# Three of seven quarter products with the operand's high and low parts side by side: one 512-column matmul for both, VectorE adds the halves

## The chip, the cores and the metric

The kernel runs on one core of one Trainium2 chip. The metric is the device time of one launch in microseconds (us). The engines have short names here: PE is TensorE (PEld its loading of weights), DVE is VectorE, ACT is ScalarE, POOL is GpSimd, SP is SyncE, which starts most transfers. PE works in 128 x 128 weights against a moving operand of up to 512 columns, and writes into eight PSUM banks of 512 fp32 columns each.

## The reference

Two decoder layers on a sequence of 512 tokens of width 1024. Each layer is a SwiGLU feed-forward block at half weight, a mixer (a convolution, a sliding-window attention and an attention to 256 memory tokens), a second feed-forward block at half weight, and a norm:

```python
def swiglu(x, w1, w3, w2):
    return (jax.nn.silu(x @ w1) * (x @ w3)) @ w2

for l in range(DEPTH):
    h = x + 0.5 * swiglu(rms_norm(x, ffn1_norm[l]), ffn1_w1[l], ffn1_w3[l], ffn1_w2[l])
    ...
    h = h + 0.5 * swiglu(rms_norm(h, ffn2_norm[l]), ffn2_w1[l], ffn2_w3[l], ffn2_w2[l])
    x = rms_norm(h, final_norm[l])
```

DEPTH is 2, D_MODEL 1024, D_FF 2816; all in fp32. The mixer, which adds to h between the two blocks, is left out here. The change lies in `x @ w1` and `x @ w3` of the four feed-forward blocks.

## The kernel before

**Numbers in two parts.** Each fp32 operand is split into a high part (a ScalarE copy into the fp32r type, L146) and a low part (VectorE subtracts the high part from the number, L147). `mm3` (L178 to L180) makes a product of two such operands by three matmuls into the same PSUM tile: high weight with high operand, high weight with low operand, low weight with high operand. Weights come as `raw` tiles by DMA from SP's queue; `pair()` gives the tiles `whi` and `wlo`, of which there are four of each.

**A feed-forward block.** The 2816 columns are 22 blocks of 128. The first four blocks are formed directly (matmuls of 512 columns into mm banks), the other 18 as nine pairs of blocks by `up_pair` (L358 to L420), a scheme of seven products of quarters in the place of eight: the contraction of 1024 is halved (two halves of four steps of 128) and the tokens are halved (QT = 256 columns). `Seven` (L295 to L343) prepares the token side once for a block: products 1, 2 and 6 take their operands from `mh` and `ml`, made by `first()`, products 3, 5, 7 and 4 from `xhi` and `xlo`, made by `rest()`; the sums of quarters are made at L321 (tile `msum`), then split: `plain` splits a quarter, `cut` a sum. Over the weight side `up_pair` loops: for both matrices (w1 and w3, index i) it splits a unit of weights, and runs two products on it, in the groups 1 and 2, 6 and 3, 5 and 7, and last product 4 for both. A product is four steps of `mm3` with 256 columns, twelve matmuls.

**Where products lie.** There are three mm banks, one cf bank, two po banks and two pt banks. In `up_pair` the list `xy` has two po banks, one for each matrix: product 1 in the left half of xy[i], product 2 in the right half; one ScalarE copy of 512 columns (L392) brings both into the SBUF tile `part[i]`, and VectorE adds them into `u` or `g` (L386, in the function `add`). Products 6 and 5 are later accumulated onto the left half of xy[i] (they start without `start`), each copied into `part[i]` by ScalarE (L400, L405). The list `zv` has two pt banks: product 3 in the left half of zv[i], products 7 and then 4 in the right. After 7, one VectorE add of 512 columns (L407 calls `add`) brings both halves into u or g with product 5's copy; after 4 one of 256. SiLU (L414), product (L415) and the split of the result (L418, L419) follow. Since `add` records its operation at one line, all of these adds, and the two that form sums of weights in `raw`, carry L386.

**Order.** `ffn` runs through QUARTERS, (0,6), (6,6), (12,6), (18,4): the stages q0 to q3 hold two, three, three and one pairs (q0 also has the four direct blocks, made ahead), each followed by a down projection of those columns, which adds into h at L506. There are four blocks, so 36 pairs. The order of the instructions on each engine isn't written by hand: a scheduler decides it from the dependencies of the program and a few `issue_after` hints, and each engine then runs its list in order, with semaphore waits. A tile or bank that is written again waits for its last readers; the program tracks a PSUM bank as one thing, so a write to its one half waits for a reader of the other.

Of the kernel before, what the change touches and what calls it, by code (L numbers as in the profile page):

```python
# [11 lines left out]
F32R = mybir.dt.float32r  # L12
I32 = mybir.dt.int32
AF = mybir.ActivationFunctionType
ALU = mybir.AluOpType
AX = mybir.AxisListType
ALL = slice(None)

P = 128
D = 1024  # L20
S = 512
# [44 lines left out]
def trunk(ctx: ExitStack, tc: tile.TileContext, xT, memT, pos, w1a, w3a, w2a, w1b, w3b, w2b,  # L66
          wconv, wqk, wvm, wmem, wout, gains, small, rows, consts, out):
    nc = tc.nc
    V, G, A, T = nc.vector, nc.gpsimd, nc.scalar, nc.tensor

    const = ctx.enter_context(tc.tile_pool(name="const", bufs=1))
    res = ctx.enter_context(tc.tile_pool(name="res", bufs=1))
# [7 lines left out]
    turn, tail, hold = [0], [None], {}  # L80
# [10 lines left out]
    def bank(shape, tag):  # L91

        if tag == "mm":
            return ps_mm.tile(shape, F32, tag=tag, name=tag)
        return ps_ax.tile(shape, F32, tag=tag, name=tag, bufs=1 if tag == "cf" else 2)

    def tm(name, tag="t", bufs=None):
        return tmp.tile([P, S], F32, tag=tag, name=name, **({"bufs": bufs} if bufs else {}))
# [4 lines left out]
    def raw_tile(src, cols):  # L103
        raw = wst.tile([P, UNIT], F32, tag="raw", name="raw", bufs=3)
        nc.sync.dma_start(raw[:, 0:cols], src)
        return raw
# [5 lines left out]
    first = []  # L112
# [32 lines left out]
    def split(hi, lo, x, on):  # L145
        a = A.activation(hi, x, AF.Copy)  # L146
        return a, on.tensor_tensor(out=lo, in0=x, in1=hi.bitcast(F32), op=ALU.subtract)  # L147
# [29 lines left out]
    def mm3(ps, a, b, first, last, **more):  # L177
        T.matmul(ps, a[0], b[0], start=first, stop=False, **more)  # L178
        T.matmul(ps, a[0], b[1], start=False, stop=False, **more)  # L179
        tail[0] = T.matmul(ps, a[1], b[0], start=False, stop=last, **more)  # L180

    def at(p, *idx):
        return tuple(x[idx] for x in p)

    def blk(k, n=P):
        return slice(k * n, (k + 1) * n)
# [57 lines left out]
    class Stat:  # L244


        def __init__(self, tag, n=S, on=None):
            self.sums, self.tag, self.n, self.on = [], tag, n, on
# [18 lines left out]
    def operand():  # L267
        return (res.tile([P, KD, S], F32R, tag="xhi", name="xhi"), res.tile([P, KD, S], F32R, tag="xlo", name="xlo"))
# [16 lines left out]
    QT = 256  # L285
# [9 lines left out]
    class Seven:  # L295


        def __init__(self, n):
            self.n = n
            self.m = {}  # L300

        def quarter(self, half, i, t):

            return self.n[2 * half + i][:, :, blk(t, QT)]

        def first(self):
            near = (res.tile([P, 3, 4, QT], F32R, tag="nsh", name="mh"), res.tile([P, 3, 4, QT], F32R, tag="nsl", name="ml"))
            for i, j in enumerate((1, 2, 6)):
                self.m[j] = at(near, ALL, i)
            self.plain(1, 0, 0)  # L310
            self.plain(2, 1, 0)
            f = self.sum((0, 1), (1, 1), ALU.subtract)
            self.sum(f, (0, 0), ALU.subtract, f)
            self.cut(6, f)
# [7 lines left out]
            return out  # L322

        def plain(self, j, half, t):
            for i in range(2):
                hi, lo = at(self.m[j], ALL, blk(i, 2))
                split(hi, lo, self.quarter(half, i, t), V)

        def cut(self, j, f):
            hi, lo = (x.rearrange("p k t -> p (k t)") for x in self.m[j])  # L330
            split(hi, lo, f, V)

        def rest(self):
            far = tuple(x.rearrange("p k (u t) -> p (k u) t", t=QT) for x in operand())
            for i, j in enumerate((3, 5, 7, 4)):
                self.m[j] = at(far, ALL, blk(i, 4))
            self.plain(3, 1, 1)
            self.cut(5, self.sum((0, 0), (0, 1), ALU.subtract))
            f = self.sum((1, 1), (0, 1), ALU.subtract)
            self.cut(7, f)  # L340
            self.sum(f, (0, 0), ALU.add, f)
            self.sum(f, (1, 0), ALU.subtract, f)
            self.cut(4, f)  # L343
# [5 lines left out]
    def gated():  # L349
        p = gated_pair()  # L350
        return [at(p, ALL, i, ALL) for i in range(2)]

    def unit(x):
        p = pair()
        split(p[0], p[1], x, V)
        return p

    def up_pair(l, w13, f, M):  # L358

        raw = [raw_tile(w13[i][l, f], D) for i in range(2)]  # L360
        X = []
        for i in range(2):

            x = wst.tile([P, UNIT], F32, tag="aux", name="wsum", bufs=3)
            nc.sync.dma_start(x.rearrange("p (f c) -> p f c", f=2), w13[i][l, f : f + 2, :, 0:QW].rearrange("f p c -> p f c"))
            G.dma_start(x, w13[i][l, f + 1], accum_op=ALU.add)
            X.append(x)
        z = wst.tile([P, UNIT], F32, tag="raw", name="raw", bufs=3)
        for i in range(2):
            nc.sync.dma_start(z[:, blk(i, QW)], w13[i][l, f + 1, :, QW:])  # L370
        xy = [bank([P, S], "po") for _ in range(2)]
        zv = [bank([P, S], "pt") for _ in range(2)]
        x0, x1 = blk(0, QT), blk(1, QT)

        def product(ps, w, half, j, first=False):


            for k in range(4):
                mm3(ps, at(w, ALL, blk(4 * half + k)), at(M.m[j], ALL, k), first and k == 0, k == 3, skip_group_check=True)

        u, g = (tmp.tile([P, 2, S], F32, tag=t, name=t, bufs=n) for t, n in (("u", 1), ("g", 2)))
        part = [tm("part", "sq", 2) for _ in range(2)]
        to = (u, g)

        def add(out, a, b):
            V.tensor_tensor(out=out, in0=a, in1=b, op=ALU.add)  # L386

        for i in range(2):
            w = unit(raw[i])
            product(xy[i][:, x0], w, 0, 1, first=True)  # L390
            product(xy[i][:, x1], w, 1, 2)
            A.activation(part[i], xy[i], AF.Copy)  # L392
            add(to[i][:, 0, x0], part[i][:, x0], part[i][:, x1])

            add(raw[i][:, 0:QW], raw[i][:, 0:QW], X[i][:, QW:])
            add(raw[i][:, QW:], raw[i][:, QW:], raw[i][:, 0:QW])
        for i in range(2):
            w = unit(raw[i])
            product(xy[i][:, x0], w, 0, 6)
            A.activation(part[i][:, x1], xy[i][:, x0], AF.Copy)  # L400
            product(zv[i][:, x0], w, 1, 3, first=True)
        for i in range(2):
            w = unit(X[i])
            product(xy[i][:, x0], w, 1, 5)
            A.activation(part[i][:, x0], xy[i][:, x0], AF.Copy)  # L405
            product(zv[i][:, x1], w, 0, 7)
            add(to[i][:, :, x1], zv[i].rearrange("p (n t) -> p n t", n=2), part[i][:, x0].unsqueeze(1).to_broadcast([P, 2, QT]))  # L407
        w = unit(z)
        for i in range(2):
            product(zv[i][:, x1], w, i, 4)  # L410
            add(to[i][:, 1, x0], zv[i][:, x1], part[i][:, x1])
        out = gated()
        for n, sign in enumerate((1.0, -1.0)):
            A.activation(u[:, n], u[:, n], AF.Silu, scale=sign)  # L414
        M.gated = V.tensor_tensor(out=g, in0=g, in1=u, op=ALU.mult)  # L415
        for n, sign in enumerate((1.0, -1.0)):
            hi, lo = out[n]
            A.activation(hi, g[:, n], AF.Copy, scale=sign)  # L418
            V.scalar_tensor_tensor(out=lo, in0=g[:, n], scalar=sign, in1=hi.bitcast(F32), op0=ALU.mult, op1=ALU.subtract)  # L419
        return out  # L420

    def ffn(l, w13, w2, x, sums, factors, last, at_product, aside=None, closing=None):
# [55 lines left out]
        for q, (f0, nf) in enumerate(QUARTERS):  # L478
            ahead = 2 if q + 1 < len(QUARTERS) else 0
            for f in range(f0, f0 + nf + ahead, 2):  # L480
                if f not in g:
                    g[f], g[f + 1] = up_pair(l, w13, f, M)
                    if f == PLAIN:
                        with tc.issue_after(M.gated.ins):
                            rescale = after()
# [615 lines left out]
    for l in range(L):  # L1101
        x, new = nxt.x, Stat("st")
# [163 lines left out]
```

## Time and profile before

| what | value |
|---|---|
| median of 3 runs | 1763.83 us (1762.75 to 1764.15) |
| the profiled execution | 1764.53 us |
| its span, first to last instruction | 1762.8 us |
| granted clock of TensorE | 0.998 |
| matmuls of 256 columns by the pt lines (L178 to L180) | 864 of each line |
| hardware DMA queue | 190.45 MB, 35.4% of 16 engines |
| software DMA queue | 61.35 MB, 19.4% of 16 engines |

All times of instructions are from the one profiled execution. A row of the timeline has the start, the duration, the engine, the line, the operation, and what goes out and in, and in square brackets the idle time of the engine before it with what ended it. A row of a group has the count, the busy time in total, the mean in ns of one, and the idle time before the group with its releasers. A row of the waits of PE has the total, how often, and the longest. Matmuls overlap in the pipeline, so that one row's duration is longer than the distance to the next.

### The profile page before, as it was taken

How to read it: one execution, taken by the hardware profiler on the slowest of the kernel's cores; microseconds unless marked ns; L12 is line 12 of the kernel's file. 1: busy time of each engine (PE TensorE's matmuls, PEld its weight loads, DVE VectorE, ACT ScalarE, POOL GpSimd, SP SyncE). 2: the span in 40 equal slices, each digit the busy share in tenths (PEclk: the TensorE clock that was granted, in tenths of full speed). 3: DMA queues.
4: the chain of work that ended last, by engine and by line, in shares of the span. 5: the costliest groups of instructions: out<-in, count | busy, mean ns of one | idle time of the engine just before them, and what ended most of it. 6: DMA issues, size and time to landing. Idle time of an engine off the chain costs nothing.

```text
span 1762.8 us, 28084 instructions
## 1 busy us (share of the span) xinstructions
PE 1746.5 (99%) x11004; PEld 1576.7 (89%) x11004; DVE 1281.3 (73%) x1898; ACT 900.7 (51%) x1373; POOL 195.6 (11%) x220
## 2 busy tenths in 40 slices
PE   8999999999999999999999999999999999999998
PEld 7989999988888989898889898989888889998987
DVE  7968666589877757575677786666898677665756
ACT  6646444355765535353655463444467654353533
POOL 1001000006121000000010010000251310000000
PEclk9999999999999999999999999999999999999999
DMA  9456645257257546465567465642671766474622
GB/s 285 120 162 171 181 133 149 65 159 177 72 105 170 146 140 170 131 166 140 155 139 183 129 181 142 168 132 79 164 172 36 155 144 166 134 185 116 169 81 84
DMA packets 97205, 253.60 MB, mean 144 GB/s; under 512 B 9904, under 2 KB 16304, under 8 KB 97072
## 3 DMA queue, kind: packets, MB, share of 16 engines
q1 hardware_dynamic: 78064, 190.45, 35.4%
q0 software_dynamic: 19008, 61.35, 19.4%
q8 instruction: 86, 1.41, 0.3%
q14 instruction: 47, 0.39, 0.1%
HBM read 249.67 MB, written 2.10 MB: 143 GB/s over the span
## 4 chain that ended last, share of the span: by engine, by line
PE 98%; DVE 1%; DMA 1%; ACT 0%; issue 0%; SPq 0%; DVEq 0%; ACTq 0%
PE mm L178 14%; PE mm L179 14%; PE mm L180 14%; PE po L178 9%; PE po L179 9%; PE po L180 9%; PE pt L178 6%; PE pt L179 6%; PE pt L180 6%; PE po L870 2%; PE mm L818 1%; PE cf L178 1%; PE cf L180 1%; PE cf L179 1%; PE pt L859 1%; DMA raw<-in_w2b 1%
## 5 line engine op out<-in xcount | busy, mean ns | idle before, releaser
L146 ACT ACTIVATE whi<-raw 128x1024 fp32r<-128x1024 f32 (+3 forms) x346 | 326.2, 946 | 440.9 <-PE mm L179 219.9
L147 DVE TENSOR_TENSOR wlo<-raw,whi 128x1024 fp32r<-128x1024 f32 (+3 forms) x346 | 376.0, 1088 | 118.9 <-ACT whi L146 118.0
L179 PE MATMUL mm<-glo,whi 128*128 128x512 f32 (+1 forms) x752 | 292.1, 388 | 0.0
L178 PE MATMUL mm<-ghi,whi 128*128 128x512 f32 (+1 forms) x752 | 291.8, 390 | 0.0
L180 PE MATMUL mm<-ghi,wlo 128*128 128x512 f32 (+1 forms) x734 | 284.9, 388 | 0.0
L178 PE MATMUL pt<-xhi,whi 128*128 128x256 f32 x864 | 243.3, 283 | 1.4 <-DVE g L386 1.4
L180 PE MATMUL po<-mh,wlo 128*128 128x256 f32 x864 | 244.5, 283 | 0.0
L179 PE MATMUL po<-ml,whi 128*128 128x256 f32 x864 | 244.5, 283 | 0.0
L178 PE MATMUL po<-mh,whi 128*128 128x256 f32 x864 | 244.4, 283 | 0.0
L180 PE MATMUL pt<-xhi,wlo 128*128 128x256 f32 x864 | 243.9, 283 | 0.0
L179 PE MATMUL pt<-xlo,whi 128*128 128x256 f32 x864 | 243.9, 283 | 0.0
L506 DVE SCALAR_TENSOR_TENSOR h<-mm,h 128x512 f32<-128x512 f32 x126 | 86.3, 688 | 132.0 <-PE mm L180 131.9
L178 PEld LDWEIGHTS pt<-xhi,whi 128*128 128x128 f32 x864 | 165.2, 192 | 2.4 <-DVE g L386 1.6
L178 PEld LDWEIGHTS mm<-ghi,whi 128*128 128x128 f32 x752 | 141.4, 188 | 28.8 <-DVE h L506 1.2
L179 PEld LDWEIGHTS pt<-xlo,whi 128*128 128x128 f32 x864 | 165.7, 192 | 0.8
L178 PEld LDWEIGHTS po<-mh,whi 128*128 128x128 f32 x864 | 165.8, 192 | 0.7
L179 PEld LDWEIGHTS po<-ml,whi 128*128 128x128 f32 x864 | 165.8, 192 | 0.6
L179 PEld LDWEIGHTS mm<-glo,whi 128*128 128x128 f32 x752 | 141.3, 188 | 27.5
L180 PEld LDWEIGHTS po<-mh,wlo 128*128 128x128 f32 x864 | 165.8, 192 | 0.0
L180 PEld LDWEIGHTS pt<-xhi,wlo 128*128 128x128 f32 x864 | 165.7, 192 | 0.0
L180 PEld LDWEIGHTS mm<-ghi,wlo 128*128 128x128 f32 x734 | 137.8, 188 | 28.5
L1000 DVE SCALAR_TENSOR_TENSOR there<-ypad,par,there 128x512 f32<-128x512 f32 x180 | 136.0, 779 | 1.3
(334 smaller groups left out, 3322.0 us busy)
## 6 DMA issues: line engine op xcount, KB each, us to landing
raw<-in_w2a SPq DMA_DIRECT2D x48, 384.0 KB, 3.5
raw<-in_w2b SPq DMA_DIRECT2D x48, 384.0 KB, 3.6
raw<-in_w1b SPq DMA_DIRECT2D x26, 512.0 KB, 3.6
raw<-in_w3b SPq DMA_DIRECT2D x26, 512.0 KB, 3.7
raw<-in_w1a SPq DMA_DIRECT2D x25, 512.0 KB, 3.6
raw<-in_w3a SPq DMA_DIRECT2D x25, 512.0 KB, 4.0
wsum<-in_w1a SPq DMA_DIRECT2D x18, 512.0 KB, 4.4
wsum<-in_w3a SPq DMA_DIRECT2D x18, 512.0 KB, 4.3
```

What stands on the lines that cost most here:

```text
L146: a = A.activation(hi, x, AF.Copy)
L147: return a, on.tensor_tensor(out=lo, in0=x, in1=hi.bitcast(F32), op=ALU.subtract)
L178: T.matmul(ps, a[0], b[0], start=first, stop=False, **more)
L179: T.matmul(ps, a[0], b[1], start=False, stop=False, **more)
L180: tail[0] = T.matmul(ps, a[1], b[0], start=False, stop=last, **more)
L506: added = V.scalar_tensor_tensor(out=h[:, d, :], in0=ps, scalar=0.5, in1=h[:, d, :], op0=ALU.mult, op1=ALU.add)
L818: tail[0] = T.matmul(pp[i][:, z, :], q, k, start=not masked, stop=True, skip_group_check=True)
L859: tail[0] = T.transpose(pt[:, i, j, :], pr[:, i, blk(j)], ident)
L870: tail[0] = T.matmul(po[:, 2 * c + i, :], ptb[:, i, j, :], v, start=(j == 0), stop=(j == nk - 1))
L1000: V.scalar_tensor_tensor(out=cv[:, c, :], in0=ypad[:, c, j : j + S], scalar=conv_w[:, c, j : j + 1], in1=cv[:, c, :], op0=ALU.mult, op1=AL ...
```

## The change

The token operands are laid out anew: for each step of 128 the high part and the low part of the 256 columns lie next to each other, in one tile. Products 2, 7 and 4 use a new function `beside`: for each step one matmul of 512 columns, high weight with high and low operand side by side (the line L392 of the changed kernel), and one of 256, low weight with high operand (L390), onto the left half. The result takes a whole bank, whose halves VectorE adds (`summed`, two adds; for product 7 a ScalarE copy and an add). Products 1, 6, 3 and 5 are made as before, by `mm3`. Product 7 now comes ahead of 5 in the program.

Since a wide product takes a whole bank, the banks are shared anew: one pt bank `x` holds products 1, 6 and 5 of both matrices, each matrix in one half; one pt bank `c` holds product 3 of both; the po banks are for product 2 and for 7 with 4. In the changed kernel the ScalarE copies are L408 (product 1), L419 (product 6), L428 (product 5) and L425 (product 7), and all adds are L399.

```diff
         def first(self):
-            near = (res.tile([P, 3, 4, QT], F32R, tag="nsh", name="mh"), res.tile([P, 3, 4, QT], F32R, tag="nsl", name="ml"))
+            near = [res.tile([P, 6, 2, QT], F32R, tag=t, name=n) for t, n in (("nsh", "mh"), ("nsl", "ml"))]
...
         def cut(self, j, f):
-            hi, lo = (x.rearrange("p k t -> p (k t)") for x in self.m[j])
-            split(hi, lo, f, V)
+            z = self.whole[j]
+            split(z[:, :, 0], z[:, :, 1], f.rearrange("p (k t) -> p k t", k=4), V)
...
-        xy = [bank([P, S], "po") for _ in range(2)]
-        zv = [bank([P, S], "pt") for _ in range(2)]
+        x = bank([P, 2, QT], "pt")
...
+        def beside(ps, w, half, j, first=False):
+            for k in range(4):
+                (hi, lo), m = at(w, ALL, blk(4 * half + k)), M.m[j][k]
+                for n in (1, 0) if k == 3 else (0, 1):
+                    if n:
+                        T.matmul(ps[:, 0], lo, m[:, 0], start=False, stop=False, skip_group_check=True)
+                    else:
+                        tail[0] = T.matmul(ps, hi, m, start=first and k == 0, stop=k == 3, skip_group_check=True)
...
+        def summed(out, ps, a):
+            add(out, ps[:, 0], a)
+            add(out, out, ps[:, 1])
+
         for i in range(2):
             w = unit(raw[i])
-            product(xy[i][:, x0], w, 0, 1, first=True)
-            product(xy[i][:, x1], w, 1, 2)
-            A.activation(part[i], xy[i], AF.Copy)
-            add(to[i][:, 0, x0], part[i][:, x0], part[i][:, x1])
+            product(x[:, i], w, 0, 1, first=not i)
+            A.activation(part[i][:, x0], x[:, i], AF.Copy)
+            y = bank([P, 2, QT], "po")
+            beside(y, w, 1, 2, first=True)
+            summed(to[i][:, 0, x0], y, part[i][:, x0])
...
+        c, v = bank([P, 2, QT], "pt"), []
         for i in range(2):
             w = unit(raw[i])
-            product(xy[i][:, x0], w, 0, 6)
-            A.activation(part[i][:, x1], xy[i][:, x0], AF.Copy)
-            product(zv[i][:, x0], w, 1, 3, first=True)
+            product(x[:, i], w, 0, 6)
+            A.activation(part[i][:, x1], x[:, i], AF.Copy)
+            product(c[:, i], w, 1, 3, first=not i)
         for i in range(2):
             w = unit(X[i])
-            product(xy[i][:, x0], w, 1, 5)
-            A.activation(part[i][:, x0], xy[i][:, x0], AF.Copy)
-            product(zv[i][:, x1], w, 0, 7)
-            add(to[i][:, :, x1], zv[i].rearrange("p (n t) -> p n t", n=2), part[i][:, x0].unsqueeze(1).to_broadcast([P, 2, QT]))
+            v.append(bank([P, 2, QT], "po"))
+            beside(v[i], w, 0, 7, first=True)
+            A.activation(to[i][:, 1, x1], v[i][:, 0], AF.Copy)
+            add(to[i][:, 1, x1], to[i][:, 1, x1], v[i][:, 1])
+            product(x[:, i], w, 1, 5)
+            A.activation(part[i][:, x0], x[:, i], AF.Copy)
+            add(to[i][:, 0, x1], c[:, i], part[i][:, x0])
+            add(to[i][:, 1, x1], to[i][:, 1, x1], part[i][:, x0])
         w = unit(z)
         for i in range(2):
-            product(zv[i][:, x1], w, i, 4)
-            add(to[i][:, 1, x0], zv[i][:, x1], part[i][:, x1])
+            beside(v[i], w, i, 4)
+            summed(to[i][:, 1, x0], v[i], part[i][:, x1])
```

How this moves the instructions shows at three places. The number behind a name tells one tile from the next of the same name; what stands in brackets is the engine whose semaphore the instruction waits for (Activation is ScalarE).

On PE, in the first stage q0, at the end of a pair's product 3 and the start of product 6 of the second matrix. Before (pt_532 is zv of the second matrix, po_530 its bank xy):

```order
L179 MATMUL pt_532<-xlo_495,whi_630 128x256
L180 MATMUL pt_532<-xhi_494,wlo_631 128x256
L178 MATMUL po_530<-mh_337,whi_630 128x256 [waits Activation_49]
L179 MATMUL po_530<-ml_338,whi_630 128x256
L180 MATMUL po_530<-mh_337,wlo_631 128x256
```

The same place in the changed kernel: the end of product 6 of the first matrix (weights whi_595) and all of product 6 of the second (whi_624), both in the bank x, pt_529, and then product 5 of the first (whi_653):

```order
L180 MATMUL pt_529<-ml_338,wlo_596 128x256
L178 MATMUL pt_529<-ml_338,whi_624 128x256 [waits Activation_49]
L179 MATMUL pt_529<-ml_338,whi_624 128x256
...
L179 MATMUL pt_529<-ml_338,whi_624 128x256
L180 MATMUL pt_529<-ml_338,wlo_625 128x256
L178 MATMUL pt_529<-xhi_494,whi_653 128x256 [waits Activation_49]
L179 MATMUL pt_529<-xhi_494,whi_653 128x256 [waits DVE_49]
```

Before, another bank's product lay between two products on one bank; now three products on x follow one another, and the second and the third wait for the ScalarE copy of the one just ahead.

On ScalarE at the same place, before (part_535 and part_536 are the tiles `part` of the two matrices):

```order
L392 ACTIVATE part_536<-po_530 128x512 [waits PE_49]
L400 ACTIVATE part_535<-po_529 128x256 [waits DVE_49,PE_49]
L146 ACTIVATE whi_719<-raw_526 128x1024 [waits DMAHW5_49,DMAHW4_49,PE_49]
L146 ACTIVATE xhi_494<-msum_505 128x1024 [waits DVE_49]
L146 ACTIVATE whi_779<-raw_758 128x1024 [waits DMAHW6_49,PE_49]
L400 ACTIVATE part_536<-po_530 128x256 [waits DVE_49,PE_49]
L405 ACTIVATE part_535<-po_529 128x256 [waits PE_49]
```

And in the changed kernel (part_532 and part_533 are the same two tiles):

```order
L408 ACTIVATE part_533<-pt_529 128x256 [waits PE_49]
L146 ACTIVATE whi_713<-raw_526 128x1024 [waits DMAHW4_49,DMAHW5_49,PE_49,Activation_49]
L419 ACTIVATE part_532<-pt_529 128x256 [waits PE_49]
L146 ACTIVATE xlo_495<-msum_505 128x4x256 [waits DVE_49]
L146 ACTIVATE whi_764<-raw_746 128x1024 [waits DMAHW6_49,PE_49,Activation_49]
L419 ACTIVATE part_533<-pt_529 128x256 [waits PE_49]
L428 ACTIVATE part_532<-pt_529 128x256 [waits PE_49,Activation_49]
```

A split of the next weights (1024 columns) stands now ahead of each of the two copies of product 6 (L419), and the split's own wait is for PE's last use of an older `whi` tile.

On PE again, in stage q2 of the first block, where one pair ends and the next begins. Before (po_2859 is xy of the next pair):

```order
L179 MATMUL pt_2620<-xlo_495,whi_2777 128x256
L180 MATMUL pt_2620<-xhi_494,wlo_2778 128x256
L178 MATMUL po_2859<-mh_337,whi_2867 128x256 [waits Activation_49]
L179 MATMUL po_2859<-ml_338,whi_2867 128x256
L180 MATMUL po_2859<-mh_337,wlo_2868 128x256 [waits DVE_49]
```

In the changed kernel (pt_2545 is the old pair's bank x, pt_2775 that of the next):

```order
L179 MATMUL pt_2545<-xhi_494,whi_2699 128x256
L180 MATMUL pt_2545<-xhi_494,wlo_2700 128x256
L178 MATMUL pt_2775<-mh_337,whi_2780 128x256 [waits Activation_49]
L179 MATMUL pt_2775<-mh_337,whi_2780 128x256
L180 MATMUL pt_2775<-mh_337,wlo_2781 128x256
```

The next pair's first product came after a product in another bank, and waited for weights; now it comes right behind product 5 of the old pair, in the same bank, and waits for the copy (L428) of that product.

More of the change, by code (lines that the diff above doesn't have):

```diff
@@ L299, in __init__ @@
             self.n = n
-            self.m = {}
+            self.m, self.ends, self.whole = {}, {}, {}
         def quarter(self, half, i, t):
@@ L306, in first @@
         def first(self):
-            near = (res.tile([P, 3, 4, QT], F32R, tag="nsh", name="mh"), res.tile([P, 3, 4, QT], F32R, tag="nsl", name="ml"))
+            near = [res.tile([P, 6, 2, QT], F32R, tag=t, name=n) for t, n in (("nsh", "mh"), ("nsl", "ml"))]
             for i, j in enumerate((1, 2, 6)):
-                self.m[j] = at(near, ALL, i)
+                self.m[j] = [near[b // 6][:, b % 6] for b in range(4 * i, 4 * i + 4)]
+                self.ends[j] = [near[b // 6][:, b % 6 : b % 6 + 2] for b in (4 * i, 4 * i + 2)]
+            self.whole[6] = near[1][:, 2:6]
             self.plain(1, 0, 0)
@@ L324, in plain @@
         def plain(self, j, half, t):
-            for i in range(2):
-                hi, lo = at(self.m[j], ALL, blk(i, 2))
-                split(hi, lo, self.quarter(half, i, t), V)
+            for i, z in enumerate(self.ends[j]):
+                split(z[:, :, 0], z[:, :, 1], self.quarter(half, i, t), V)
         def cut(self, j, f):
-            hi, lo = (x.rearrange("p k t -> p (k t)") for x in self.m[j])
-            split(hi, lo, f, V)
+            z = self.whole[j]
+            split(z[:, :, 0], z[:, :, 1], f.rearrange("p (k t) -> p k t", k=4), V)
         def rest(self):
-            far = tuple(x.rearrange("p k (u t) -> p (k u) t", t=QT) for x in operand())
+            far = [x.rearrange("p k (u t) -> p k u t", t=QT) for x in operand()]
             for i, j in enumerate((3, 5, 7, 4)):
-                self.m[j] = at(far, ALL, blk(i, 4))
+                z = self.whole[j] = far[i // 2][:, blk(i % 2, 4)]
+                self.m[j], self.ends[j] = [z[:, k] for k in range(4)], [z[:, 0:2], z[:, 2:4]]
             self.plain(3, 1, 1)
@@ L378, in product @@
             for k in range(4):
-                mm3(ps, at(w, ALL, blk(4 * half + k)), at(M.m[j], ALL, k), first and k == 0, k == 3, skip_group_check=True)
+                m = M.m[j][k]
+                mm3(ps, at(w, ALL, blk(4 * half + k)), (m[:, 0], m[:, 1]), first and k == 0, k == 3, skip_group_check=True)
+        def beside(ps, w, half, j, first=False):
[6 more added lines that the diff above has]
+                        tail[0] = T.matmul(ps, hi, m, start=first and k == 0, stop=k == 3, skip_group_check=True)
         u, g = (tmp.tile([P, 2, S], F32, tag=t, name=t, bufs=n) for t, n in (("u", 1), ("g", 2)))
```

## The prediction

> **What bounds the kernel now.** I read the page first, then the waits of PE, then busy time by stretch, and last the timeline.
>
> ```profile
> PE 1746.5 (99%) x11004; PEld 1576.7 (89%) x11004; DVE 1281.3 (73%) x1898; ACT 900.7 (51%) x1373; POOL 195.6 (11%) x220
> PE 98%; DVE 1%; DMA 1%; ACT 0%; issue 0%; SPq 0%; DVEq 0%; ACTq 0%
> PE mm L178 <- ACT xhi L156: 6.0, 1, 6.0
> PE pt L178 <- DVE g L386: 1.4, 1, 1.4
> ```
>
> The first two lines are from the page (busy time, and the chain of work that ended last); the other two are the two longest waits of PE. PE is busy for 1746.5 of 1762.8 us and the chain is 98% PE: the time is the sum of the matmuls, and every microsecond in which PE newly waits is added in full. Of the pairs' matmuls (tiles po and pt) one alone waited, for 1.4 us.
>
> Which engine comes next is a matter of the stage. The rows below give busy time in four stretches of pairs: stage q0 of the first FFN (two pairs), q1 of the same FFN (three), q2 (three, as ordinary stages look) and q0 of the second FFN.
>
> ```profile
> 54.70:92.50 37.80, 37.80 (x315) 37.68 (x314) 33.96 (x44) 24.00 (x34) 3.45 (x4) 1.00 0.59 160
> 139.40:202.40 63.00, 63.00 (x517) 62.52 (x516) 53.59 (x103) 37.25 (x59) 8.34 (x8) 1.00 0.69 175
> 232.70:295.80 63.10, 63.10 (x516) 62.56 (x516) 42.56 (x53) 33.62 (x49) 4.32 (x5) 1.00 0.67 170
> 577.20:614.90 37.70, 37.70 (x314) 37.61 (x313) 32.72 (x42) 23.53 (x34) 3.45 (x4) 1.00 0.58 143
> ```
>
> Behind the length of the stretch stand PE, the weight loads, VectorE, ScalarE and GpSimd, then the granted clock and the DMA share. VectorE has 34.0 of 37.8 us (90%) in q0 and 42.6 of 63.1 (67%) in q2; ScalarE has 24.0 and 33.6.
>
> **The matmuls that go.** PE's rows are pipelined, so the price of one is the distance between two starts.
>
> ```profile
> 66.00 0.28 PE L179 MATMUL po<-ml,whi 128*128 128x256 f32 x1
> 66.12 0.28 PE L180 MATMUL po<-mh,wlo 128*128 128x256 f32 x1
> 66.24 0.28 PE L178 MATMUL po<-xhi,whi 128*128 128x256 f32 x1
> ...
> 295.96 0.40 PE L178 MATMUL mm<-ghi,whi 128*128 128x512 f32 x1
> ...
> 297.35 0.39 PE L178 MATMUL mm<-ghi,whi 128*128 128x512 f32 x1
> ...
> 305.51 0.39 PE L178 MATMUL mm<-ghi,whi 128*128 128x512 f32 x1
> ```
>
> 256 columns take 0.120 us. The rows from 295.96 on are 512 columns wide, without a gap: 36 steps from 297.35 to 305.51, 0.227 us each, while the six right behind the change from narrow to wide (295.96 to 297.35) took 0.232. A step of a changed product was 3 x 0.120 = 0.360 us; wide and narrow in turn it is now 0.227 + 0.120 = 0.347 or 0.232 + 0.120 = 0.352, and saves 0.013 or 0.008. I take the middle, 0.010, since the trace has no such alternation. Products 2, 7 and 4, each for two matrices, with four steps: 24 steps in a pair, 864 in 36 pairs: **8.6 us** (6.9 to 11.2; 0 if the alternation costs more). Each step drops one instruction and no columns, 768 pass PE either way, and hence the gain is this small. The Trainium skill ("TensorE: Matmul & The Clock Gate", Back-to-back issue gap) gives for a single matmul at full clock N/2.4 + 2.5 ns, so 2.5 ns for the dropped instruction. By that, an estimate, the gain would be 864 x 2.5 ns = 2.2 us; the trace's 120 and 227 ns, at clock 1.00, speak for more: 3 x 120 - 227 - 120 = 13 ns.
>
> **The wait that is added.** Before, the products 1, 6 and 5 of matrix 1 and of matrix 3 lay in two po banks. Now both share one pt bank x, each in its half, and the program lets PE write the one half only when ScalarE has copied out the other. In the order, PE gets three products on x in a row in the first q0 (product 6, 6, 5), each with a wait for ScalarE. What stands behind such a wait on PE is everything: PE runs in order, so no matmul fills the gap.
>
> The price, by the shortest case, comes from four rows: from PE's last matmul to its reader, and from a reader's end to PE.
>
> ```profile
> 79.20 0.28 PE L180 MATMUL pt<-xhi,wlo 128*128 128x256 f32 x1
> 79.52 0.43 DVE L386 TENSOR_TENSOR u<-pt,part 128x256 f32<-128x256 f32 x1 [0.63 <-PE pt L180]
> ...
> 1492.96 0.68 DVE L386 TENSOR_TENSOR g<-pt,part 128x512 f32<-128x512 f32 x1
> 1493.69 0.39 PE L178 MATMUL pt<-xhi,whi 128*128 128x256 f32 x1 [1.38 <-DVE g L386]
> ...
> L400 ACT ACTIVATE part<-po 128x256 f32<-128x256 f32 x72 | 27.3, 381 | 69.2 <-PE po L180 68.1 <-DVE u L386 0.8 <-DVE g L386 0.3
> ```
>
> The reader starts 0.32 us after the last matmul's start; ScalarE's copy takes 0.38; PE starts 0.05 after its reader's end (1493.64). The next matmul would have started 0.12 after the last one, so the **short price** is 0.32 + 0.38 + 0.05 - 0.12 = 0.63 us. The trace shows the return path for VectorE alone; I take it for ScalarE too, with 0 and 0.3 as bounds, which moves 21 places by -1 and +5 us.
>
> Often ScalarE is not free. Its split of the next weights also waits for this product, but for the one before the last of its matmuls, so it gets in first. The trace of before has the very case:
>
> ```profile
> 66.32 1.06 ACT L146 ACTIVATE whi<-raw 128x1024 fp32r<-128x1024 f32 x1 [0.27 <-PE po L179]
> 67.28 0.37 ACT L400 ACTIVATE part<-po 128x256 f32<-128x256 f32 x1
> ```
>
> The product ended with the matmul of 66.12 above; its copy ended at 67.65. In before PE went on at 66.24 in another bank. Now it would go on at 67.65 + 0.05 = 67.70: the **long price** is 1.46 us.
>
> Places where a product on x follows directly the one whose copy it waits for: 21 in the order of the change, none before. Three stand in each of the four q0 stages, nine in the q1 and q2 stages, none in q3.
> - q0: in each stage two have the split of 1024 columns in front on ScalarE, one is bare: 4 x (2 x 1.46 + 0.63) = 14.2 us.
> - q1 and q2, eight stages: one direct place each, at the pair's end, bare (0.63); other products on x come four or eight steps behind their copy's product, where a split in front on ScalarE can cost from 0 to 0.83 (the long price less the short). I take 0.83 once in a stage, ScalarE being busy over half the time there: 8 x 1.46 = 11.7, and 0.6 for the ninth place: 12.3.
>
> The Trainium skill ("PSUM — Partial Sum Buffer", PSUM bank collisions raise a hardware error) says that two engines must never touch one bank's partitions at once, disjoint columns included, and that the wait is to be set by bank: by that rule the wait is no excess of the scheduler and speaks against this sharing; without it the sum would be the gain alone. No run here tests the collision.
>
> **What VectorE gets.** A pair had four adds of 256 columns and two of 512; now it has 14 of 256.
>
> ```profile
> 73.00 1.22 DVE L147 TENSOR_TENSOR wlo<-raw,whi 128x1024 fp32r<-128x1024 f32 x1
> 74.14 0.68 DVE L386 TENSOR_TENSOR g<-pt,part 128x512 f32<-128x512 f32 x1
> 74.74 0.68 DVE L386 TENSOR_TENSOR raw<-raw 128x512 f32<-128x512 f32 x1
> 75.33 1.22 DVE L147 TENSOR_TENSOR xlo<-msum,xhi 128x1024 fp32r<-128x1024 f32 x1
> ...
> L386 DVE TENSOR_TENSOR g<-part 128x256 f32<-128x256 f32 x36 | 15.0, 416 | 0.0
> ```
>
> A 512 add takes 0.60 of VectorE's time (74.14 to 74.74, 0.08 less than its row). The 256 add, 0.42, less the same 0.08, takes 0.34: 10 x 0.34 - 2 x 0.60 = 2.2 us more in a pair, 79 in all. In q2 that is 42.6 + 6.6 of 63: covered by PE. In q0 it is 34.0 + 4.4 = 38.4, against 37.8 - 0.6 + 3.6 = 40.8 with the new waits: VectorE just fits, but work before product 4's matmuls comes later. The low half of product 4's operand (75.33, ended 76.55) was needed by PE at 78.0, 1.45 us of room; four more adds stand ahead of it and PE is not later by more than two waits. I count 0.5 in each of two FFN1 q0 stages and 1.0 in q1 of the first FFN, where VectorE had 53.6 of 63.0 and gets 60.2: 2 us, bounds 0 and 12 (half of the adds of these eleven pairs, 11 x 1.1). Operands laid out hi beside lo are read and written in runs of 256; no row shows a difference, and none is counted (bounds +-0.1 us for each of 16 cuts, in VectorE's slack). ScalarE has four copies of 256 more and two of 512 less, 0.4 us in a pair, beside PE.
>
> **Sum.** 14.2 + 12.3 + 2.0 - 8.6 = +19.9 us on the profiled execution's 1764.5, which lies 0.7 above the runs' median of 1763.8: 1783.7, rounded down to 1783, since the 11.7 of q1 and q2 is an upper choice.
>
> **Rivals.** *All waits short.* ScalarE does the copies ahead of its splits, or the splits are held up by something else: 21 x 0.63 = 13.2 against 8.6, +4.6: 1768.4; with the gain at 11.2 it is +2.0 and 1765.8, no change that can be measured. For it: half the places are bare in the order. Against: the rows at 66.32 and 67.28.
> *The waits cost less than the matmuls save.* This is the case of faster: it decides at 8.6 / 21 = 0.41 us for a place (0.53 with the gain at 11.2). If the copies were out in time everywhere, 1763.8 - 8.6 = 1755.2, or 1752.6. For it: in before such copies never delayed PE, and the return path to PE is from a single row. Against: 0.38 of copy and 0.28 of the last matmul's own duration are in every place.
> *VectorE becomes the bound in q0 and in q1 of the first FFN.* If half of the 24 us of adds in these eleven pairs come uncovered, +12 less the 2 that are counted: 1783.7 + 10 = 1794. For it: 38.4 us of work in 40.8. Against: waits of PE and of VectorE overlap.
> *The wide matmul saves nothing* (a gain of 0): 1783.7 + 8.6 = 1792.
>
> **How the numbers follow.** Forecast, 1770 to 1791: 0.66. All waits short, 1763 to 1770: 0.12. Faster, 1750 to 1762: 0.12. VectorE or no gain, 1790 to 1803: 0.10. The time is that of the first: 1783. The range from 1764 to 1792 takes in the first, nearly all of the second and a little of the last, 0.80. A measurement of this kernel tells about 0.2% (3.5 us) from no change: faster 0.12, same 0.08, slower 0.80.
>
> **What would show it.** PE's waits after the change should name ScalarE's copies L408, L419 and L428 as releasers for pt, some 21 to 35 times, from 0.6 to 1.5 us, about 26 us in all; the wide-narrow step should repeat at 0.347 to 0.352; q0 stretches should grow to about 41 us and q3 stay. It is wrong if PE's idle time grows by under 9 us, if the waits name VectorE, or if the step is 0.360.

## The result and the profile after

| kernel | median, us | runs | ratio to before, 95% interval |
|---|---|---|---|
| before | 1763.42 (1762.75 to 1764.15) | 5 | |
| the change | 1812.62 (1810.34 to 1815.04) | 5 | 1.0278 [1.0263, 1.0293] |

The change is slower by 49 us. Its profiled execution took 1812.62 us, with a span of 1810.9. The page of the change, its busy time:

```profile
PE 1760.7 (97%) x10140; PEld 1536.0 (85%) x10140; DVE 1365.1 (75%) x2186; ACT 908.6 (50%) x1445; POOL 195.0 (11%) x220
```

PE has 864 matmuls fewer, as it should, VectorE 84 us more. PE stood idle for 1810.9 - 1760.7 = 50.2 us, where it was 16.3; the rest of the longer span counts as busy time, the slow matmuls of q3 that are shown below among it. The waits of PE in the change say for what it stood idle (total, times, longest):

```profile
PE mm L178 <- ACT ghi L441: 11.9, 4, 3.0
PE pt L178 <- ACT part L419: 8.4, 6, 1.6
PE pt L178 <- ACT part L428: 8.2, 13, 1.4
PE mm L178 <- ACT xhi L156: 6.3, 1, 6.3
PE pt L178 <- ACT part L408: 3.9, 9, 0.8
```

Lines 2, 3 and 5 are the waits on the shared bank x that were forecast: 28 times, 20.5 us. The first line was not: four waits of 3 us for `ghi`, the high part of a pair's result, and all four are in q3. The fourth line is the wait at the start, which was there before. Two more waits of 0.7 us each, in q0 of the third block, belong to the same kind: a small matmul of the norm takes its pt bank there between two products, and waits for product 5's copy (L428), and the next product waits for the copy of that matmul's result.

One look at two of the forecast places and at one in q3, from the timeline of PE in the change:

```profile
66.47 0.28 PE L180 MATMUL pt<-ml,wlo 128*128 128x256 f32 x1
68.10 0.39 PE L178 MATMUL pt<-ml,whi 128*128 128x256 f32 x1 [1.35 <-ACT part L419]
68.33 0.28 PE L179 MATMUL pt<-ml,whi 128*128 128x256 f32 x1
...
283.10 0.28 PE L180 MATMUL pt<-xhi,wlo 128*128 128x256 f32 x1
283.85 0.38 PE L178 MATMUL pt<-mh,whi 128*128 128x256 f32 x1 [0.47 <-ACT part L428]
...
359.29 0.40 PE L180 MATMUL mm<-ghi,wlo 128*128 128x512 f32 x1
362.67 1.23 PE L178 MATMUL mm<-ghi,whi 128*128 128x512 f32 x3 [2.99 <-ACT ghi L441]
363.70 0.63 PE L179 MATMUL mm<-glo,whi 128*128 128x512 f32 x1
364.13 0.63 PE L180 MATMUL mm<-ghi,wlo 128*128 128x512 f32 x1
...
366.26 0.55 PE L179 MATMUL mm<-glo,whi 128*128 128x512 f32 x1
366.65 0.39 PE L180 MATMUL mm<-ghi,wlo 128*128 128x512 f32 x1
```

Where nothing waits, the distances are 0.12 and 0.23 us. The first place lost 68.10 - 66.47 - 0.12 = 1.51 us and 0.11 more at its second matmul; the second lost 0.63. In q3, PE lost 3.15 us, and then 0.43 us from matmul to matmul in place of 0.23, for 3 us.

What makes `ghi` late in q3 is in the timelines of ScalarE and VectorE at that place:

```profile
358.67 0.63 ACT L146 ACTIVATE whi<-raw 128x512 fp32r<-128x512 f32 x1 [1.30 <-PE pt L179]
359.21 0.37 ACT L428 ACTIVATE part<-pt 128x256 f32<-128x256 f32 x1
359.34 0.69 DVE L147 TENSOR_TENSOR wlo<-raw,whi 128x512 fp32r<-128x512 f32 x1 [2.82 <-ACT whi L146]
359.95 0.42 DVE L399 TENSOR_TENSOR g<-pt,part 128x256 f32<-128x256 f32 x1
360.28 0.42 DVE L399 TENSOR_TENSOR g<-g,part 128x256 f32<-128x256 f32 x1
360.73 1.23 DVE L438 TENSOR_TENSOR g<-g,u 128x1024 f32<-128x1024 f32 x1
361.99 1.15 ACT L441 ACTIVATE ghi<-g 128x512 fp32r<-128x512 f32 x2 [2.42 <-DVE g L438]
```

Product 5 of the second matrix is now the pair's last: it has to come behind the copy of the other half of x, and the scheduler put product 4 and 14 of the 18 matmuls of the down projection that need nothing of this pair ahead of it. Behind it stand a copy, two adds, the product with the SiLU and the split, 4.2 us from its last matmul (358.47) to PE's restart, with the other four matmuls to cover them. Splits of weights stand in front of the copy (358.67) and of the first add (359.34) and make each of the two 0.3 to 0.4 us later. Before, product 4 was last, and all 18 matmuls stood behind it (18 x 0.23 = 4.1 us):

```profile
345.94 0.28 PE L180 MATMUL pt<-xhi,wlo 128*128 128x256 f32 x1
346.06 0.40 PE L178 MATMUL mm<-ghi,whi 128*128 128x512 f32 x1
...
349.94 0.39 PE L180 MATMUL mm<-ghi,wlo 128*128 128x512 f32 x1
350.17 0.84 PE L178 MATMUL mm<-ghi,whi 128*128 128x512 f32 x3
```

The row of 350.17 is the first that needs this pair, and it had nothing to wait for.

### The profile page after: what moved, and what is told of

Read it like the earlier page. It is cut to its first block, busy times and chain, and to the rows that moved or that the text cites. A ratio compares the mean times of both kernels' runs of the same rounds, so it can differ in the third digit from the quotient of the medians.

```text
span 1810.9 us, 26624 instructions
## 1 busy us (share of the span) xinstructions
PE 1760.7 (97%) x10140; PEld 1536.0 (85%) x10140; DVE 1365.1 (75%) x2186; ACT 908.6 (50%) x1445; POOL 195.0 (11%) x220
## 5 line engine op out<-in xcount | busy, mean ns | idle before, releaser
L178 PE MATMUL mm<-ghi,whi 128*128 128x512 f32 (+1 forms) x752 | 295.5, 395 | 11.9 <-ACT ghi L441 11.9
L392 PE MATMUL po<-xlo,whi 128*128 128x512 f32 x576 | 208.2, 398 | 0.5 <-DVE xlo L147 0.5
L178 PEld LDWEIGHTS mm<-ghi,whi 128*128 128x128 f32 x752 | 142.6, 190 | 42.1 <-ACT ghi L441 13.7
L529 DVE SCALAR_TENSOR_TENSOR h<-mm,h 128x512 f32<-128x512 f32 x126 | 86.5, 689 | 120.3 <-PE mm L180 120.2
L178 PE MATMUL pt<-xhi,whi 128*128 128x256 f32 x576 | 163.1, 283 | 5.7 <-ACT part L419 3.0
L179 PE MATMUL pt<-xhi,whi 128*128 128x256 f32 x576 | 162.9, 283 | 0.0
L180 PE MATMUL pt<-xhi,wlo 128*128 128x256 f32 x576 | 162.6, 282 | 0.0
L390 PE MATMUL po<-xlo,wlo 128*128 128x256 f32 x576 | 138.5, 281 | 0.0
L392 PEld LDWEIGHTS po<-xlo,whi 128*128 128x128 f32 x576 | 105.0, 189 | 13.9 <-DVE xlo L147 0.7
L390 PEld LDWEIGHTS po<-xlo,wlo 128*128 128x128 f32 x576 | 108.9, 189 | 8.8
L178 PEld LDWEIGHTS pt<-xhi,whi 128*128 128x128 f32 x576 | 109.0, 189 | 8.1 <-ACT part L419 3.4
L178 PE MATMUL mm<-xhi,whi 128*128 128x512 f32 x272 | 108.6, 403 | 6.8 <-ACT xhi L156 6.3
L179 PEld LDWEIGHTS pt<-xhi,whi 128*128 128x128 f32 x576 | 109.1, 189 | 4.3
L180 PEld LDWEIGHTS pt<-xhi,wlo 128*128 128x128 f32 x576 | 109.0, 189 | 0.0
L180 PE MATMUL mm<-xhi,wlo 128*128 128x512 f32 x272 | 106.8, 393 | 0.0
```

Of the source, the lines that this page charges most:

```text
L390: T.matmul(ps[:, 0], lo, m[:, 0], start=False, stop=False, skip_group_check=True)
L392: tail[0] = T.matmul(ps, hi, m, start=first and k == 0, stop=k == 3, skip_group_check=True)
L529: added = V.scalar_tensor_tensor(out=h[:, d, :], in0=ps, scalar=0.5, in1=h[:, d, :], op0=ALU.mult, op1=ALU.add)
```

## The experiments

Where each kernel lost or won time, by stage, in its profiled execution. A stage's end is the last add into h (L506 before, L529 in the change); the numbers are us by which the stretch from one end to the next is longer than before, summed over the four blocks. q0 includes what lies ahead of it. A profiled execution isn't the median one: it took 1775.03 us in e1 (median 1778.16), 1758.86 in e3 (1757.24) and 1796.75 in e2 (1798.83). Each diff is against the change, in e3 and e6 against the kernel before, and each shows only the lines that matter.

| kernel | q0 | q1 | q2 | q3 | all |
|---|---|---|---|---|---|
| the change | 17.5 | 6.0 | 5.7 | 18.8 | 48.0 |
| e1 banks by matrix | 11.9 | 0.7 | -2.8 | 0.7 | 10.5 |
| e2 narrow, shared | 12.2 | 1.5 | 0.4 | 18.1 | 32.2 |
| e3 wide only | -1.1 | -1.0 | -2.8 | -0.8 | -5.7 |
| e4 four last | 14.9 | 6.0 | 6.3 | 8.8 | 36.0 |
| e8 mixed | -2.0 | -1.0 | -1.8 | -0.1 | -4.9 |
| e9 no second adds | 14.7 | -1.0 | -2.5 | 18.6 | 29.8 |

### e1: the banks shared by matrix

```diff
-        x = bank([P, 2, QT], "pt")
+        x = [bank([P, 2, QT], "pt") for _ in range(2)]
-            product(x[:, i], w, 0, 1, first=not i)
+            product(x[i][:, 0], w, 0, 1, first=True)
...
-            product(c[:, i], w, 1, 3, first=not i)
+            product(x[i][:, 1], w, 1, 3)
```

> The change with its seven products, wide matmuls and adds of VectorE as they are; only the two pt banks are shared in another way: one bank for each matrix, with products 1, 6, 5 in its left half and product 3 in its right, so that between two products on one bank lies one on another bank. Theory A (the sharing of bank x costs the time, by its waits and by the order it gives in q3): waits of PE in the pairs fall from about 27 us to under 3, the idle time of 3 us in front of q3's down projections goes, and the time is that of before less the gain, 1763.4 - 6 = 1757 (1754 to 1761). Theory B (the ten more adds of VectorE in a pair, or the operands in runs of 256, cost it): the time stays above 1790. Both in part: 1765 to 1785.

Measured: 1778.16 us, 1.0077 [1.0063, 1.0090]. The waits for the copies are gone but for 0.7 us, and q3 is within 1 us of before. So the sharing between the matrices carries 34 of the 49 us. But theory A's 1757 is missed by 21 us: PE now waits for VectorE, in q0 and in q1 of the first block, as the waits of PE in this kernel show:

```profile
PE po L392 <- DVE xlo L147: 7.5, 5, 2.5
PE mm L178 <- ACT xhi L156: 6.3, 2, 5.9
PE pt L180 <- DVE wlo L147: 2.5, 4, 1.2
```

xlo here is the operand of product 4, made late; the second line is the start of the kernel. Neither theory alone holds.

### e2: narrow products in the banks of the change

```diff
-                for n in (1, 0) if k == 3 else (0, 1):
...
+                mm3(ps[:, 0], at(w, ALL, blk(4 * half + k)), (m[:, 0], m[:, 1]), first and k == 0, k == 3, skip_group_check=True)
...
-            add(out, out, ps[:, 1])
```

> Banks, copies and program order of the change, but products 2, 7 and 4 by three matmuls of 256 columns as before; the add of the second half is left out, since there is none. VectorE has six adds of 256 columns less in a pair (2.0 us) than the change. Theory A: the waits on x and the idle time in q3 stay as in the change and the gain of about 6 us goes: 1812.6 + 6 = 1818 (1808 to 1824). Theory B (adds): near before, 1763 to 1772, since the adds are gone. Theory C (wide matmuls cost more than they look): near before, too.

Measured: 1798.83 us, 1.0196 [1.0183, 1.0210]. By itself the sharing costs 35 us: q3 loses what it lost in the change, q0 12.2 of its 17.5. So the loss in q3 needs neither the wide matmuls nor the second adds. But q1 and q2, with 1.5 us a stage in the change, lost almost nothing: all theories missed this. Either the width or the adds bring the waits there; e9 tells them apart.

### e3: wide products in the banks of before

```diff
-            product(xy[i][:, x1], w, 1, 2)
+            beside(xy[i], w, 1, 2)
...
-            product(zv[i][:, x1], w, 0, 7)
+            beside(zv[i], w, 0, 7)
...
-            product(zv[i][:, x1], w, i, 4)
+            beside(zv[i], w, i, 4)
```

> The kernel before, its banks, copies and adds, with the operands laid out hi beside lo and products 2, 7 and 4 by a matmul of 512 and one of 256 columns into the whole of the bank that they had half of. VectorE doesn't add the two halves, and the low part's half goes onto the other product of the bank. This times the gain alone. Theory A: 864 steps at 0.354 in place of 0.360 us, measured in the trace of the change: -5.2 us, and 1758 (1756 to 1760). By the prediction's 0.010 a step: -8.6, 1755. Theory C (operands in runs of 256 or the mixing of widths cost something elsewhere): 1763 or more.

Measured: 1757.24 us, 0.9961 [0.9948, 0.9973]. The gain alone is 7.0 us (1764.20 - 1757.24, before in the same set of runs), or 8.1 ns a step. The steps themselves, from PE's timeline of this kernel:

```profile
56.84 0.40 PE L392 MATMUL po<-mh,whi 128*128 128x512 f32 x1
57.08 0.28 PE L390 MATMUL po<-mh,wlo 128*128 128x256 f32 x1
57.19 0.40 PE L392 MATMUL po<-mh,whi 128*128 128x512 f32 x1
...
58.02 0.40 PE L392 MATMUL po<-ml,whi 128*128 128x512 f32 x1
58.26 0.28 PE L178 MATMUL po<-mh,whi 128*128 128x256 f32 x1
```

Four steps in 58.26 - 56.84 = 1.42 us, 0.355 each: 5 ns under 0.360 by this product. Over the whole of this trace a wide matmul takes 0.235 us on average where a narrow one follows, and that narrow one 0.118: a step of 0.353, which saves 0.0075, or 6.5 us in 864. The interval of the ratio, 4.8 to 9.2 us, has room for the forecast's 8.6 as well. No cost of operands in runs of 256 shows in the time.

### e4: product 4 of the last pair held behind product 5

```diff
+            with queued() if f == NF - 2 else nullcontext():
-            beside(v[i], w, i, 4)
+                beside(v[i], w, i, 4)
```

> The change, with product 4 of the last pair of each block held behind product 5 by a hint, so that q3 ends as before on product 4 and the 18 matmuls of the down projection that need nothing of the last pair stand behind it again. Theory A: the four idle times of 3.15 us and the slow 2 us behind each go, -20 us, but products 6, 5 and 5 on x now follow one another in q3 and add two to three waits of 0.75 us in each block, +6 to +9: 1798 (1795 to 1802). Theory D (the idle time in q3 comes from VectorE being behind with its adds, not from the order): the idle time stays and the time is 1810 or more.

Measured: 1800.22 us, 1.0207 [1.0191, 1.0223], 12.4 under the change. The wait for `ghi` is gone from the waits of PE, so it was the order; q3 keeps 2.2 us a block from the products on x that now follow one another. The mean granted clock is 0.998 again; it was 0.994 in the change.

### e5: wide products only where VectorE has room

```diff
+        wide = f >= QUARTERS[1][0] + 2 and (f >= QUARTERS[2][0] + 2 or l > 0 or w13[0] is not w1a)
...
+            if not wide:
+                return product(ps[:, 0], w, half, j, first)
```

> The banks by matrix as in e1; products 2, 7 and 4 wide only in the 25 pairs of stages in which VectorE has room, and by three matmuls without the added adds in the eight pairs of q0 and the three of q1 in the first block of the first layer. If e1 lost its time to VectorE being late in just those stages: no waits of PE for VectorE there, and the gain of the 25 pairs, 25 / 36 of the 7 us of e3, so 4.9: 1759 (1757 to 1762), faster than before. If e1 lost it to its banks (product 3 and 5 in one bank): 1770 or more.

Measured: 1769.03 us, 1.0043 [1.0029, 1.0056]: missed by 10 us, and close to the 1770 that stood for the banks. The profiled execution was the slowest, with 1775.20. q0 has nearly VectorE's work of before here, and yet PE waits there for product 4's operand (4.5 us, four times, longest 2.1). In VectorE's timeline of this kernel and of before, this split and its neighbours:

```profile
76.75 0.68 DVE L403 TENSOR_TENSOR raw<-raw 128x512 f32<-128x512 f32 x1
78.04 0.69 DVE L403 TENSOR_TENSOR raw<-raw,wsum 128x512 f32<-128x512 f32 x1 [0.61 <-DVE raw L403]
78.64 1.22 DVE L147 TENSOR_TENSOR xlo<-msum,xlo 128x1024 fp32r<-128x1024 f32 x1
```

```profile
75.33 1.22 DVE L147 TENSOR_TENSOR xlo<-msum,xhi 128x1024 fp32r<-128x1024 f32 x1
76.47 0.69 DVE L386 TENSOR_TENSOR raw<-raw,wsum 128x512 f32<-128x512 f32 x1
```

The new bank plan made the scheduler put both of the next pair's sums of weights (`raw`) ahead of it; before, the second stood behind. So in q0 the place of that one split in VectorE's list counts, not the sum of its work alone. e10 tests it, and e8 goes back to the order of before there. The bank plan also costs in another way: three times, 2.2 us in all, a product's start in a pt bank waited for an add that reads this bank (PE pt L178 for DVE g L403), all in q1.

### e6: more adds on the kernel before

```diff
+            for _ in range(2):
-            add(to[i][:, 0, x0], part[i][:, x0], part[i][:, x1])
+                add(to[i][:, 0, x0], part[i][:, x0], part[i][:, x1])
...
+            for n in (0, 1, 1):
+                add(to[i][:, n, x1], zv[i][:, blk(n, QT)], part[i][:, x0])
```

> The kernel before with nothing else than more adds on VectorE: each add after product 2 and 4 is made twice (the same numbers to the same place), and the one of 512 columns after 5 and 7 becomes three of 256, so that a pair has 14 adds of 256 as in the change. If VectorE's adds alone cost what stands between e3 and e1 (21 us): 1764 + 18 to 21 = 1783 (1777 to 1788), with the waits in q0 and in q1 of the first block and none in q2 and q3. If PE covers them as the prediction had it: 1764 to 1767.

Measured: 1791.54 us, 1.0156 [1.0141, 1.0172], 8 us over the forecast, and not in the stages that it named: q2 has 2.0 us a stage. The longest of its waits of PE says why it can't stand for the change:

```profile
PE pt L178 <- DVE u L386: 11.3, 8, 1.7
```

Product 4 is accumulated in the half bank that the adds after product 7 read. Three adds there in place of one hold back product 4 itself. The change has no such wait, so e6 shows another way to lose and gives no price for the change's adds.

### e7: PE's idle time in q3 partly filled

```diff
+                if not ahead and not d:
+                    idle, (hi, lo) = bank([P, S], "cf"), begun[2][1]
+                    for n in range(6):
+                        with queued():
+                            tail[0] = T.matmul(idle, hi[:, blk(0)], g[f0][0], start=n == 0, stop=n == 5)
```

> The change, with six matmuls of 512 columns into the free cf bank, which nobody reads, at the place where PE stands idle for 3.15 us in q3. They fill 1.4 us and leave 1.8 of idle time; the chain that PE waits for is not touched. If the nine matmuls at half speed behind each of the four waits (0.43 in place of 0.23 us) come from the length of PE's idle time: they go, and the time falls by 4 x 1.9 = 7.6 us, to 1805 (1803 to 1808). If they come from something else at that place (the weights, the adds into h): the same as the change, 1811 to 1814.

Measured: 1806.12 us, 1.0244 [1.0230, 1.0258], 6.5 under the change with 7.6 forecast. PE's timeline of this kernel at the place:

```profile
360.60 0.98 PE L178 MATMUL mm<-ghi,whi 128*128 128x512 f32 x3 [1.62 <-ACT ghi L441]
361.42 0.41 PE L179 MATMUL mm<-glo,whi 128*128 128x512 f32 x1
361.66 0.40 PE L180 MATMUL mm<-ghi,wlo 128*128 128x512 f32 x1
361.90 0.40 PE L178 MATMUL mm<-ghi,whi 128*128 128x512 f32 x1
```

After 1.6 us of idle time the distances are 0.24 from the second matmul on, in all four blocks. So the slow stretch goes with the idle time and not with what is computed there.

### e8: two ways to form a pair

```diff
+        if f >= QUARTERS[2 if w13[0] is w1a else 1][0] + 2:
+            x = [bank([P, 2, QT], "pt") for _ in range(2)]
...
+        else:
+            xy = [bank([P, S], "po") for _ in range(2)]
+            zv = [bank([P, S], "pt") for _ in range(2)]
```

> Two ways to form a pair: the banks, order and adds of before (operands hi beside lo) in the fourteen pairs of stages where VectorE works over 75% (q0 of all blocks, q1 of the first block of a layer), and the wide products in banks by matrix as in e1 in the other 22. If the wide products pay where VectorE has room and the banks are not shared between matrices: 22 x 24 steps at 7.0 us / 864 = 4.3 us under before, 1759 (1757 to 1762). If VectorE's order, which was late for product 4 in e5's q0 stages even without the adds, was not the cause there: 1766 or more.

Measured in eleven runs: 1761.25 us, 0.9987 [0.9978, 0.9995]. It is the one kernel with all its adds that is under before, by 2.0 us of the 4.3 forecast (0.9 to 3.9 by the interval). By stages its profiled execution, at 1759.71 the fastest of its runs, has -4.9. VectorE works 35.1 of the 37.8 us of the first q0, and PE never waits for it there.

### e9: the second adds left out

```diff
-            add(out, out, ps[:, 1])
...
-            add(to[i][:, 1, x1], to[i][:, 1, x1], v[i][:, 1])
```

> The change, with the adds of the low part's half left out (six of 256 columns in a pair); wide matmuls, banks and copies as in the change. Against e2 it differs in the wide matmuls alone. If the adds of VectorE decide how the scheduler orders the pairs in q1 and q2, and so whether products on x follow one another there: as e2 less the gain of 7 us, 1792 (1789 to 1796), with no waits on x in q1 and q2 and those of q0 and q3 as before. If the widths decide it: 1805 or more, with 1.5 us in each of these stages.

Measured: 1792.93 us, 1.0166 [1.0152, 1.0180], as the first reading has it. q1 and q2 are at the gain alone (-1.0 and -2.5), with the wide products in place. The adds, not the widths, bring the change's waits there, and they cost 1812.6 - 1792.9 = 20 us in all. In the order without these adds, no product on x in a stage q2 follows directly the one whose copy it waits for; with them product 1 of the next pair comes right behind product 5 once in a stage.

### e10: the split for product 4 first

```diff
+            with tc.issue_after(M.four.ins) if f == PLAIN + 2 else nullcontext():
-            add(raw[i][:, 0:QW], raw[i][:, 0:QW], X[i][:, QW:])
-            add(raw[i][:, QW:], raw[i][:, QW:], raw[i][:, 0:QW])
+                add(raw[i][:, 0:QW], raw[i][:, 0:QW], X[i][:, QW:])
+                add(raw[i][:, QW:], raw[i][:, QW:], raw[i][:, 0:QW])
```

> As e1 (banks by matrix, all products wide, all adds), with one hint: in q0 the next pair's sums of weights on VectorE stand behind the split of product 4's operand. If VectorE's order makes product 4 late in q0 in e1: its wait for xlo goes, up to 2.5 us in each of four q0 stages, -6 to -9 us with restarts, 1770 (1767 to 1774). If VectorE's amount of work is the limit, the wait comes back at the next pair's weights: 1776 to 1780, as e1.

Measured: 1773.62 us, 1.0052 [1.0037, 1.0068], 4.5 under e1 at the slow end of the forecast. The wait for xlo falls from 7.5 to 2.9 us and doesn't go; 1.9 us for VectorE's adds come in its place. So the order counts in q0; whether the rest is the amount of VectorE's work or still its order, no run tells apart.

## Why the prediction was wrong in size

The direction and the waits on x were right, the size was not: +19.9 us forecast, 48 in the profile, and the range ended at 1792. What the sharing does to the end of a block was not in the forecast at all.

- **The wide matmuls**: forecast -8.6 (bounds 6.9 and 11.2), measured -7.0 in e3. By the steps of e3's trace (0.353 us) a wide matmul costs a little more than the rows right behind a change of width showed (0.235 for 0.232), so the middle was somewhat high. In the change the gain is smaller still: in stage q2 of the second block the 72 changed steps took 25.65 us, against 25.92 for 72 of 0.360, 0.27 for the 0.72 that the forecast has; no run says why.
- **The waits on x, directly behind**: long price 1.46, measured 1.51; short price 0.63, measured 0.63. Their sum with the near ones was 14.2 + 12.3 = 26.5. Measured are 28 waits of 20.5 us by the view of waits, which counts from the modelled end of the matmul before; in distances a place has 0.16 more (1.51 for 1.35, 0.63 for 0.47), so about 20.5 + 28 x 0.16 = 25.0. The sum held, in part by luck: by distances q0 has 15.4 (14.2 forecast) and q1 with q2 9.4 (12.3), where the copies of product 1 cost 0.53 a place and not the 0.83 that was taken, and the two waits around the norm's matmul stand outside the sum. Not counted was the second matmul behind each wait, 0.10 to 0.11 late: 28 x 0.1 = 3 us.
- **The step that failed: "none in q3"**. The forecast counted places at which a product on x directly follows the one whose copy it waits for, and took q3 for untouched, at -1.0 with the gain. q3 lost 18.8. There the scheduler had filled the gap with the down projection's matmuls, so that no direct place shows in the order; but these 18 matmuls were the cover for the chain from the pair's last product to `ghi`, and product 4, which has the shorter chain, went ahead of product 5. Four times 3.15 us, and four times about 1.6 us at half speed behind it (6.5 us in all by e7). e4 shows the order to be the cause, e7 the cost of the slow stretch, and e2 and e9 lose the same 18 us there without the second adds. The 14 matmuls of the down projection ahead of product 5, and the four behind it, stood in the order of the change.
- **VectorE**: 2.0 was counted, with 12 as the upper bound. Without the adds the change is 20 us faster (e9). In the change little of this is a wait for VectorE (1.2 us by name): the adds moved the scheduler's order, and by stages they cost 2.8 us in q0 and 15 in q1 and q2. With the banks by matrix PE does wait for VectorE, in q0 and in q1 of the first block. There e1 is 21 us over e3, but not by the adds alone: e5, without the second adds in these stages, is only 9 us under e1, and the rest goes with the bank plan and its order. So the rival on VectorE named the place where the adds hurt with other banks, not where they hurt in the change. The part in q1 and q2 was in the forecast by its places, as waits on x, though with the adds' order as the cause behind it; the 20 us here and the waits above overlap.
- **The stages**: forecast, by the terms and the gain of 0.24 us a pair, were 13.3 in q0 (17.5 measured), 7.5 in q1 and q2 (11.7), -1.0 in q3 (18.8). Of the missing 28 us, 20 are q3's.
- **The rivals**: "all waits short" and "faster" fall; "the wide matmul saves nothing" falls with e3.

What stays open: how the 8 us that q0, q1 and q2 have over the forecast divide among the late second matmuls, the smaller gain and VectorE; what the bank plan of e1 costs without the adds; and why e8's median keeps only half of the gain that its profile shows.

## What to carry to other kernels

Two independent streams that share a PSUM bank are tied together by every copy out of it: a bank shared by two matrices cost 35 us here (e2). With the same halves shared by the products of one matrix (e1) PE waited 0.7 us for copies, though that kernel lost 14 us against before in other ways. When a wait is added and a scheduler chooses the order, don't look only where the wait shows in the order: where the scheduler fills the gap, ask what the filling was covering before. And before adding work to an engine with 70 to 90% of a stage, read in its list what stands ahead of the one result that the bound engine needs next, since the place of that result counts beside the sum.

## What the runs showed of the hardware

After a wait of 3.0 us, TensorE in the change gave 0.43 us from start to start for 512 columns, against 0.23, until some 3.8 us after the restart (362.67 to about 366.5), and then full speed; after 1.35 us, and in e7 after 1.62, it gave full speed from the second matmul on. Four such waits lowered the mean granted clock of the execution from 0.998 to 0.994. The Trainium skill ("TensorE: Matmul & The Clock Gate", Part 1: The HAM clock gate (the "warmup" mystery)) has this as a gate that halves the clock after an idle window of about 3.4 us and opens after as much of busy time; the trace agrees on the half and nearly on the time to open (3.8), and here 3.0 us by the view of waits, 3.4 from the last matmul's start, was enough.

But the length of one wait doesn't decide it alone. Of the twelve waits of 2.98 or 2.99 us for `ghi` in the change, e2 and e9, ten were followed by half speed and two were not (e2 in the first block, at 359.19, and e9 in the second, at 876.22). Of two waits of 2.5 us in e1 the one at 80.22 was and the one at 958.98 was not, and in e10 one of 1.50 us, at 76.96, was, with a wait of 0.47 us three us ahead of it.

A wait costs PE more than its length: at all 28 places on x the matmul behind the waiting one came about 0.10 us late (0.22 from start to start in place of 0.12).
